# A gated short convolution beside attention: from channels in the rows to tokens in the rows

## The chip, the cores and the metric

One Trainium2 chip, and of it one core. The metric is the device time of one execution in microseconds. TensorE (PE in the profile) multiplies, VectorE (DVE), ScalarE (ACT) and GpSimd (POOL) do the elementwise work, and SyncE (SP) issues the weight loads.

## The reference

One decoder sub-layer over 256 tokens and a width of 2048, all in float32. The input is normalised and projected by one wide matrix; the columns feed a latent attention of 16 heads and a gated convolution of 3 taps. Both results are projected, merged by sigmoid gates, projected once more, normalised and added to the input.

```python
h = _rmsnorm(x, pre_norm_g)
proj = jnp.einsum('bsd,de->bse', h, w_in)
...
attn = attn.reshape(b, s, MLA_WIDTH) * jax.nn.silu(z_mla)
y_mla = jnp.einsum('bse,ed->bsd', attn, w_o_mla)

u = c_gate * c_in
u_pad = jnp.pad(u, ((0, 0), (CONV_K - 1, 0), (0, 0)))
conv = sum(conv_w[k] * u_pad[:, k:k + s] for k in range(CONV_K))
y_conv = jnp.einsum('bse,ed->bsd', b_gate * conv * jax.nn.silu(z_conv), w_o_conv)

merged = jax.nn.sigmoid(g_mla) * y_mla + jax.nn.sigmoid(g_conv) * y_conv
out = jnp.einsum('bsd,de->bse', merged, w_out)
x = x + _rmsnorm(out, post_norm_g)
```

## The kernel before

**Numbers in two halves.** Every float32 operand of a matmul is split into a high part (rounded to the matmul's type) and a low part (the rest): `split_act` writes the high part on ACT and the low part on DVE. A product is then three matmuls, high x high, high x low and low x high. `product` issues them one by one. `halves` puts the two halves of the activations side by side (`x_both`, 512 columns for 256 tokens), so that one matmul of 512 columns with the high weights and one of 256 with the low weights do the same; `whole` adds the two halves of the result.

**Weights.** They come in units of 128 x 2048 numbers (1 MB), loaded by SP into three `raw` buffers in the order of the list `plan`, and are split in halves of 1024 columns into five `whi` and five `wlo` buffers. `take(u)` hands out a unit and sees to it that the next one is split and three are loaded.

**Order.** TensorE's instructions stand in the order of the text (`keep_in_program_order`), and so do a few others. The rest of each engine's queue is ordered by the library's scheduler with a simulated timeline. `keep_in_program_order` queues an instruction behind the one written before it on its engine.

**Stages.** First the latents `qa` and `ckv` and the rotary key, with the normalisation of the input. Then 16 heads. For each head: the gate `z`; the attention's scores (`scores`), the turning of the probabilities (`turn`) and the values (`values`), and every head half a group of per-head projections (`group_a`, `group_b`); and between these four projections of 128 convolution channels, `cg`, `ci`, `b` and `c` in the profile (c_gate, c_in, b_gate, z_conv). Channels stand in the rows, tokens in the columns, so a shift in time is an offset in the columns: `u` has two zero columns ahead, and the three taps are one ACT and two DVE instructions. `cv_f` holds the result. In head 0 `latent_turn` transposes the latents between `z` and the first convolution unit.

Then the merged stage, `tokens(c, n, cols)`: for four blocks of 512 output columns the two gates (n = 0, 1, from `x_both`), the attention's output projection (n = 2, from `at_both`) and the convolution's (n = 3, from `cv_both`), with tokens in the rows; `features` turns the merged block. In the first block `split_branch` splits attention (n = 0) and convolution (n = 1). Last the output projection (`out`).

**Banks.** Of the eight accumulator banks, four rotate under `mm`, and `sm`, `sc`, `tp` and `o` are one each: for head 0's `ckv` transposes (`sm`, `sc`), scores, transposed probabilities and values.

Of the kernel before, what the change touches and what calls it, by code (L numbers as in the profile page):

```python
# [44 lines left out]
for _name, _n in (  # L45
    ("pre_g", KD), ("q_g", KR), ("kv_g", KR),
    ("cw0", KD), ("cw1", KD), ("cw2", KD), ("freq", 1), ("sign", 1),
):
    PV[_name] = (_at, _n)
    _at += _n  # L50
# [29 lines left out]
@with_exitstack  # L80
def tile_layer(ctx: ExitStack, tc: tile.TileContext, xw, x, pos, pvec, post_g, wc, wi, wkr, wqk, wrv, wsq, out):
    nc = tc.nc
# [13 lines left out]
    row_r = [top.tile([P, LINE], F32, name=f"frr{t}")[:, :1] for t in range(NT)]  # L96
    top.tile([P, 120], F32, name="top_pad")
    wpool = ctx.enter_context(tc.tile_pool(name="wpool", bufs=1))
# [5 lines left out]
    def add(ap, width=UNIT):  # L104
        plan.append((ap, width))
        return len(plan) - 1

    n_wi = 0

    def add_wi():  # L110
        nonlocal n_wi
        n_wi += 1
        return add(wi[n_wi - 1])

# [14 lines left out]
    for i, j in order:  # L129
        if j == "a":  # L130
            u_grp[i][0] = add(wqk[i])
        elif j == "b":
            u_grp[i][1] = add(wrv[i], 3 * HALF // 2)
        else:
            u_head[i][j] = add_wi()

# [119 lines left out]
    nc.scalar.activation(warm[:, :], mhalf[:, :], AF.Sigmoid)  # L256
    idle = bank("idle", tag="sm", bufs=1)
    for _ in range(9):
# [20 lines left out]
    kr = bp.tile([P, 2, S], F32R, name="kr")  # L279
    bp.tile([P, 4 * LINE], F32, name="bp_pad")  # L280
    mask = bp.tile([P, 3 * P], F32, name="mask")
# [60 lines left out]
    def input_rows(dgs):  # L342

        rb = bank("rb", tag="sm", bufs=1)
        for t in range(NT):
            matmul(rb[:, t * P : (t + 1) * P], ones[:, :], dgs[t][:, :], start=True, stop=True)
        nc.scalar.activation(r_x[:, :], rb[:, :S], AF.Copy)
# [103 lines left out]
    def latent_turn(name, both, g, tags):  # L451
        f = lat_f[name]
        for j2 in range(2):
            ps = bank(f"lt_{name}{j2}", tag=tags[j2], bufs=1)
            for j in range(2):
                for t in range(NT):
                    o, b = j * S + t * P, 2 * j2 + j
                    transpose(ps[:, o : o + P], f[:, t, b * P : (b + 1) * P], ident[:, :])
            for j in range(2):
                b, src = 2 * j2 + j, ps[:, j * S : (j + 1) * S]  # L460
                nc.scalar.activation(both[:, b, :S], src, AF.Copy, scale=col(g, b))
                nc.vector.scalar_tensor_tensor(
                    both[:, b, S:], src, col(g, b), both[:, b, :S].bitcast(F32), op0=ALU.mult, op1=ALU.subtract
                )
# [62 lines left out]
    def group_b(g):  # L527
        qr, vv = temp("qr", (P, HG, S), F32R), pair("vv", (P, NT, HG * DV), 2)
        w = take(u_grp[g][1])
        f = narrow(f"qr{g}", w, 0, qa)  # L530
        rope(f[:, :], f[:, :])
        for j in range(HG):

            own, other = (slice(DR * i, DR * i + DR) for i in (j, 1 - j))
            split_act(qr[own, j, :], qr[other, j, :], f[own, :])
        for t in range(NT):
            ps = bank(f"vv{g}_{t}")
            for k in range(KR):
                c = [ckv[:, k, o + t * P : o + (t + 1) * P] for o in (0, S)]
                product(ps[:, :S], c, w(2 + k, HG * DV), k == 0, k == KR - 1)  # L540
            split_act(vv[0][:, t, :], vv[1][:, t, :], ps[:, :S])
        groups[g] += [qr, vv]

    def scores(h):

        qn, kn, qr, _ = groups[h // HG]
        j = h % HG
        sc = bank(f"sc{h}", tag="sc", bufs=1)
        t0, t1 = slice(0, P), slice(P, S)
# [9 lines left out]
        if h == 0:  # L559
            temp("pad", (P, 3 * LINE), bufs=1)  # L560
        p = temp("p", (P, 3 * P), bufs=1)
# [23 lines left out]
    def turn(h, p):  # L585

        tp = bank(f"tp{h}", tag="tp", bufs=1)
        for b in range(3):
            transpose(tp[:, b * P : (b + 1) * P], p[:, b * P : (b + 1) * P], ident[:, :])
        pt = temp("pt", (P, 2, 3 * P), F32R, 1)  # L590
        split_act(pt[:, 0, :], pt[:, 1, :], tp[:, : 3 * P])
        return pt
# [15 lines left out]
    def silu(name, ps):  # L608
        f, s = temp("sl_f", bufs=1), temp(name, bufs=2 if name == "sz" else 1)
        whole(f[:, :], ps)  # L610
        rows(f[:, :])
        nc.scalar.activation(s[:, :], f[:, :], AF.Sigmoid)
        nc.vector.tensor_tensor(s[:, :], f[:, :], s[:, :], op=ALU.mult)
        return s

    def values_next(h):

        g, second = divmod(h, HG)
        if g + 1 < NG:
            (group_b if second else group_a)(g + 1)  # L620

    for h in range(H):
        uz, ug, ui, ub, uc = u_head[h]
        sz = silu("sz", project(uz, f"z{h}"))
        if h == 0:
            latent_turn("qa", qa, "q_g", ("tp", "o"))
            latent_turn("ckv", ckv, "kv_g", ("sm", "sc"))
            next(table_parts)
            key_rope()
        else:  # L630
            if h == 1:
                values(0, pt, sz0)
            p = scores(h)
        cg = temp("cg", bufs=1)
        whole(cg[:, :], project(ug, f"cg{h}"))
        rows(cg[:, :])
        if h == 0:
            group_a(0)
            group_b(0)
        u = temp("u", (P, S + 2), bufs=1)  # L640
        nc.gpsimd.memset(u[:, :2], 0.0)
        whole(u[:, 2:], project(ui, f"ci{h}"))
        nc.vector.tensor_tensor(u[:, 2:], u[:, 2:], cg[:, :], op=ALU.mult)
        rows(u[:, 2:])
        if h > 0:
            pt = turn(h, p)
        c = temp("c", bufs=1)
        nc.scalar.activation(c[:, :], u[:, :S], AF.Copy, scale=col("cw0", h))
        for i in (1, 2):
            nc.vector.scalar_tensor_tensor(  # L650
                c[:, :], u[:, i : i + S], col(f"cw{i}", h), c[:, :], op0=ALU.mult, op1=ALU.add
            )
        b = temp("b", bufs=1)
        whole(b[:, :], project(ub, f"b{h}"))
        nc.vector.tensor_tensor(c[:, :], b[:, :], c[:, :], op=ALU.mult)
        rows(c[:, :])
        if h > 0:
            values(h, pt, sz)
            values_next(h)
        else:  # L660
            p = scores(h)
        sg = silu("sg", project(uc, f"c{h}"))
        nc.vector.tensor_tensor(cv_f[:, h, :], c[:, :], sg[:, :], op=ALU.mult)
        if h == 0:
            values_next(h)
            pt, sz0 = turn(h, p), sz
# [7 lines left out]

    def split_branch(both, f, i):

        for h in (4 * i, 4 * i + 2):
            hs = slice(h, h + 2)
            split_act(both[:, hs, :S], both[:, hs, S:], f[:, hs, :], True)

    def tokens(c, n, cols):

        pss = [bank(f"sq{c}_{n}_{t}") for t in range(NT)]
        for kk in range(4):
            w = take(u_d[c][n][kk])
            if c == 0 and n < 2:
                split_branch(*((at_both, at_f), (cv_both, cv_f))[n], kk)
            for t in range(NT):
                for k4 in range(4):
                    k = 4 * kk + k4  # L690
                    a = [cols[:, k, o + t * P : o + (t + 1) * P] for o in (0, S)]
                    product(pss[t][:, :], a, w(k4, 512), k == 0, k == KD - 1)
        return pss
# [4 lines left out]
    def features(c, m, m_both):  # L698

        for t in range(NT):  # L700
            tp = bank(f"mt{c}_{t}", tag=("tp", "o")[t], bufs=1)
            for j in range(4):
                transpose(tp[:, j * P : (j + 1) * P], m[t][:, j * P : (j + 1) * P], ident[:, :])
            ks, ts = slice(4 * c, 4 * c + 4), slice(t * P, (t + 1) * P)
            lo = slice(t * P + S, (t + 1) * P + S)
            split_act(m_both[:, ks, ts], m_both[:, ks, lo], tp[:, :].rearrange("p (k q) -> p k q", k=4))

    waiting = m_both = None
    for c in range(4):
        gates = []  # L710
        for n in range(2):
            pss = tokens(c, n, x_both)
            if c == 0 and n == 1:
                fstack.close()
                merged_pool = ctx.enter_context(tc.tile_pool(name="merged_pool", bufs=1, side="right"))
                m_both = merged_pool.tile([P, KD, 2 * S], F32R, name="m_both")
            if waiting is not None:
# [8 lines left out]
        m = gates[0]  # L726
        pss = tokens(c, 2, at_both)
        for t in range(NT):
            nc.vector.tensor_tensor(m[t][:, :], pss[t][:, :], m[t][:, :], op=ALU.mult)
# [160 lines left out]
```

## Time and profile before

| | |
|---|---|
| median of 3 runs | 1058.01 us (1057.88 to 1059.24) |
| the profiled execution | 1058.48 us, span 1056.7 us |
| granted TensorE clock | 0.998 |
| heads (about 53 to 610 us) | 557 us |
| merged stage (610 to 961 us) | 351 us |
| output projection and end (961 to 1056.7 us) | 96 us |

The span is the time from the first to the last instruction; the execution's own time has a little around it. In the groups of the profile a row reads: line, engine, operation, written tile <- read tiles, shapes, count, busy time, mean time of one in ns, and the idle time before them with what ended it. In the chain of waits a row is start, length and what ran. `PEld` is the loading of TensorE's stationary operand, which overlaps the matmuls.

### The profile page before, as it was taken

How to read it: one execution, taken by the hardware profiler on the slowest of the kernel's cores; microseconds unless marked ns; L12 is line 12 of the kernel's file. 1: busy time of each engine (PE TensorE's matmuls, PEld its weight loads, DVE VectorE, ACT ScalarE, POOL GpSimd, SP SyncE). 2: the span in 40 equal slices, each digit the busy share in tenths (PEclk: the TensorE clock that was granted, in tenths of full speed). 3: DMA queues.
4: the chain of work that ended last, by engine and by line, in shares of the span. 5: the costliest groups of instructions: out<-in, count | busy, mean ns of one | idle time of the engine just before them, and what ended most of it. 6: DMA issues, size and time to landing. Idle time of an engine off the chain costs nothing.

```text
span 1056.7 us, 14237 instructions
## 1 busy us (share of the span) xinstructions
PE 1047.0 (99%) x5510; PEld 903.2 (85%) x5510; DVE 706.1 (67%) x1114; ACT 587.9 (56%) x858; POOL 44.1 (4%) x107
## 2 busy tenths in 40 slices
PE   9999999999999999999999999999999999999997
PEld 8888888988889888898888888888888888888885
DVE  7589877877878768778787766455554455445562
ACT  7777566666656666666665665334444434433450
POOL 7610000000000000000000000000000000000000
PEclk9999999999999999999999999999999999999999
DMA  8745454554545545454454555555555555558542
GB/s 341 303 166 189 160 200 150 199 199 150 180 171 192 187 166 195 167 188 174 176 188 171 187 175 197 198 199 175 189 194 199 197 187 187 187 199 308 190 179 80
DMA packets 29860, 201.81 MB, mean 191 GB/s; under 512 B 3360, under 2 KB 4064, under 8 KB 7392
## 3 DMA queue, kind: packets, MB, share of 16 engines
q1 hardware_dynamic: 29232, 197.54, 52.2%
q10 hardware_dynamic: 432, 3.33, 0.8%
q8 instruction: 43, 0.70, 0.3%
q14 instruction: 25, 0.20, 0.1%
q0 software_dynamic: 128, 0.03, 0.0%
HBM read 198.79 MB, written 2.10 MB: 190 GB/s over the span
## 4 chain that ended last, share of the span: by engine, by line
PE 98%; issue 1%; DVE 1%; POOL 0%; ACT 0%; POOLq 0%; DVEq 0%; ACTq 0%
PE sq L86 33%; PE ci L86 8%; PE b L86 8%; PE z L86 8%; PE c L86 8%; PE cg L86 8%; PE out L86 7%; PE vv L86 2%; PE qa L86 2%; PE ckv L86 2%; PE kn L86 2%; PE qn L86 2%; PE sc L86 1%; PE qr L86 1%; PE o L86 1%
## 5 line engine op out<-in xcount | busy, mean ns | idle before, releaser
L231 DVE TENSOR_TENSOR wlo<-raw,whi 128x1024 fp32r<-128x1024 f32 (+1 forms) x370 | 436.7, 1198 | 226.8 <-ACT whi L230 189.7
L230 ACT ACTIVATE whi<-raw 128x1024 fp32r<-128x1024 f32 (+1 forms) x372 | 383.6, 1035 | 334.2 <-PE sq L86 184.8
L86 PE MATMUL sq<-whi,x_both 128*128 128x512 f32 x512 | 159.0, 390 | 0.0
L86 PEld LDWEIGHTS sq<-whi,x_both 128*128 128x128 f32 x512 | 96.1, 188 | 19.8
L86 PE MATMUL sq<-wlo,x_both 128*128 128x512 f32 x256 | 99.6, 389 | 0.0
L86 PE MATMUL sq<-whi,cv_both 128*128 128x512 f32 x256 | 79.4, 389 | 0.0
L86 PE MATMUL sq<-whi,at_both 128*128 128x512 f32 x256 | 79.4, 389 | 0.0
L86 PE MATMUL out<-whi,m_both 128*128 128x512 f32 x256 | 79.3, 390 | 0.0
L86 PE MATMUL b<-x_both,whi 128*128 128x512 f32 x256 | 62.5, 396 | 0.0
L86 PE MATMUL z<-x_both,whi 128*128 128x512 f32 x256 | 61.2, 391 | 0.0
L86 PE MATMUL ci<-x_both,whi 128*128 128x512 f32 x256 | 61.1, 391 | 0.0
L86 PE MATMUL c<-x_both,whi 128*128 128x512 f32 x256 | 61.0, 390 | 0.0
L86 PE MATMUL cg<-x_both,whi 128*128 128x512 f32 x256 | 60.8, 390 | 0.0
L86 PEld LDWEIGHTS sq<-whi,cv_both 128*128 128x128 f32 x256 | 48.1, 188 | 10.0
L86 PEld LDWEIGHTS sq<-whi,at_both 128*128 128x128 f32 x256 | 48.1, 188 | 10.0
L86 PEld LDWEIGHTS out<-whi,m_both 128*128 128x128 f32 x256 | 48.1, 188 | 9.9
L86 PEld LDWEIGHTS sq<-wlo,x_both 128*128 128x128 f32 x256 | 48.1, 188 | 9.9
L86 PEld LDWEIGHTS ci<-x_both,whi 128*128 128x128 f32 x256 | 47.0, 188 | 9.2
L86 PEld LDWEIGHTS b<-x_both,whi 128*128 128x128 f32 x256 | 46.9, 188 | 9.3
L86 PEld LDWEIGHTS z<-x_both,whi 128*128 128x128 f32 x256 | 47.0, 188 | 9.1
L86 PEld LDWEIGHTS c<-x_both,whi 128*128 128x128 f32 x256 | 47.0, 188 | 9.1
L86 PEld LDWEIGHTS cg<-x_both,whi 128*128 128x128 f32 x256 | 47.0, 188 | 8.9
(223 smaller groups left out, 1550.6 us busy)
## 6 DMA issues: line engine op xcount, KB each, us to landing
raw<-wi_dram SPq DMA_DIRECT2D x80, 1024.0 KB, 4.8
raw<-wsq_dram SPq DMA_DIRECT2D x80, 1024.0 KB, 4.8
raw<-wqk_dram SPq DMA_DIRECT2D x8, 1024.0 KB, 4.8
raw<-wrv_dram SPq DMA_DIRECT2D x8, 768.0 KB, 4.1
raw<-wc_dram SPq DMA_DIRECT2D x4, 1024.0 KB, 10.0
cv_f<-x_dram SPq DMA_DIRECT2D x1, 2048.0 KB, 9.4
xr<-x_dram ACTq DMA_DIRECT2D x1, 2048.0 KB, 11.4
raw<-xw_dram SPq DMA_DIRECT2D x5, 384.0 KB, 6.0
```

The costliest lines, as they stand in the source:

```text
L86: return tc.keep_in_program_order(nc.tensor.matmul(*a, **kw))
L230: a = nc.scalar.activation(hi, src, AF.Copy)
L231: b = nc.vector.tensor_tensor(lo, src, hi.bitcast(F32), op=ALU.subtract)
```

## The change

The convolution's projections are made with tokens in the rows. Four heads share a block of 512 channels, and head h does one of the block's four projections, c_gate, c_in, z_conv and b_gate in turn: `channels(h, i)` takes its unit i (of 4) at the place where one of the four old projections stood, into two `cv` banks, one for each 128 tokens. `channels_done` evicts and multiplies as the projections come. Once u = c_gate * c_in is there, `taps` moves it down by one and by two rows with DMAs from POOL's queue, fetches the tap weights as rows broadcast to all partitions, and sums up, in steps (`yield`) that the loop calls later in the next head, with the sums on DVE kept in program order. In the merged stage `turn_branch` transposes the result on TensorE, at n = 1 and 2 of the first block, in place of the splits at n = 1.

The banks become four `mm`, two `cv`, one `st` (scores, transposed probabilities, and what used `sm`) and `o`; `latent_turn` uses `st` and `o` for `qa` and the two `cv` for `ckv`. Some tiles have one buffer instead of two, padding tiles change, and the tap weights leave the first small load `pvec`. The weight units keep their number, size and order; those of the convolution are laid out as the merged stage's.

```diff
-            u_head[i][j] = add_wi()
+            u_head[i][j] = add(wcv[i, j - 1] if j else wz[i])
...
-        qr, vv = temp("qr", (P, HG, S), F32R), pair("vv", (P, NT, HG * DV), 2)
+        qr, vv = temp("qr", (P, HG, S), F32R, 1), pair("vv", (P, NT, HG * DV))
...
-        sc = bank(f"sc{h}", tag="sc", bufs=1)
+        sc = bank(f"sc{h}", tag="st", bufs=1)
...
-        tp = bank(f"tp{h}", tag="tp", bufs=1)
+        tp = bank(f"tp{h}", tag="st", bufs=1)
...
+    cv_t = cv_f[:, :, :].rearrange("p (j t k) s -> p j t (k s)", j=4, t=NT)
+    cv_ps = {}
+
+    def channels(h, i):
+        if i == 0:
+            cv_ps["now"] = [bank(f"cv{h}_{t}", tag="cv", bufs=2) for t in range(NT)]
+        w = take(u_head[h][1 + i])
+        for t in range(NT):
+            for k4 in range(4):
+                k = 4 * i + k4
+                a = [x_both[:, k, o + t * P : o + (t + 1) * P] for o in (0, S)]
+                product(cv_ps["now"][t][:, :], a, w(k4, 512), k == 0, k == KD - 1)
+        if i == 3:
+            channels_done(*divmod(h, 4))
+
+    def channels_done(j, n):
+        for t in range(NT):
+            ps, r = cv_ps["now"][t], r_col[:, t : t + 1]
+            w, u = cv_w[:, t, :], cv_t[:, j, t, :]
+            if n == 0:
+                nc.scalar.activation(u, ps[:, :], AF.Copy, scale=r)
+            elif n == 2:
+                nc.scalar.activation(w, ps[:, :], AF.Sigmoid, scale=r)
+            if n:
+                dst = u if n == 1 else w
+                nc.vector.scalar_tensor_tensor(dst, ps[:, :], r, dst, op0=ALU.mult, op1=ALU.mult)
+            if n == 3:
+                nc.vector.tensor_tensor(u, u, w, op=ALU.mult)
+
+    def taps(j, t):
+        u, parts = cv_t[:, j, t, :], []
+        for d in (1, 2):
+            m = temp(f"mv{d}", (P, 512), bufs=1, tag=f"mv{d}x")
+            if t:
+                nc.gpsimd.dma_start(out=m[:d, :], in_=cv_t[P - d :, j, 0, :])
+            else:
+                nc.gpsimd.memset(m[:d, :], 0.0)
+            nc.gpsimd.dma_start(out=m[d:, :], in_=u[: P - d, :])
+            parts.append(m[:, :])
+        def tap(d):
+            cw = temp("cw", (P, 512), bufs=2)
+            nc.gpsimd.dma_start(out=cw[:, :], in_=cwr[2 - d : 3 - d, 512 * j : 512 * (j + 1)].to_broadcast([P, 512]))
+            return cw
+
+        def join(dst, a, b, op):
+            tc.keep_in_program_order(nc.vector.tensor_tensor(dst, a, b, op=op))
+
+        cws = [tap(d) for d in (1, 2)]
+        yield
+        for a, cw in zip(parts, cws):
+            join(a, a, cw[:, :], ALU.mult)
+        join(parts[0], parts[0], parts[1], ALU.add)
+        cw = tap(0)
+        yield
+        join(u, u, cw[:, :], ALU.mult)
+        join(u, u, parts[0], ALU.add)
+        yield
...
     for h in range(H):
...
         if h == 0:
-            latent_turn("qa", qa, "q_g", ("tp", "o"))
-            latent_turn("ckv", ckv, "kv_g", ("sm", "sc"))
+            latent_turn("qa", qa, "q_g", (("st", 1), ("o", 1)))
+            latent_turn("ckv", ckv, "kv_g", (("cv", 2), ("cv", 2)))
...
             p = scores(h)
-        cg = temp("cg", bufs=1)
-        whole(cg[:, :], project(ug, f"cg{h}"))
-        rows(cg[:, :])
+        channels(h, 0)
...
+        channels(h, 1)
         if h > 0:
             pt = turn(h, p)
...
+        if h % 4 > 1:
+            next(tap)
+        channels(h, 2)
         if h > 0:
             values(h, pt, sz)
+            if h % 4 > 1:
+                next(tap)
             values_next(h)
...
+        channels(h, 3)
+        if h % 4 in (1, 2):
+            tap = taps(h // 4, 2 - h % 4)
+            next(tap)
...
+    def turn_branch(i):
+        j, t = divmod(i, NT)
+        turned(f"ct{i}", cv_t[:, j, t, :], cv_both, j, t)
+
+    def turned(name, src, both, c, t):
+        tp = bank(name, tag=("st", "o")[t], bufs=1)
+        for j in range(4):
+            transpose(tp[:, j * P : (j + 1) * P], src[:, j * P : (j + 1) * P], ident[:, :])
+        ks, ts = slice(4 * c, 4 * c + 4), slice(t * P, (t + 1) * P)
+        lo = slice(t * P + S, (t + 1) * P + S)
+        split_act(both[:, ks, ts], both[:, ks, lo], tp[:, :].rearrange("p (k q) -> p k q", k=4))
...
-            if c == 0 and n < 2:
-                split_branch(*((at_both, at_f), (cv_both, cv_f))[n], kk)
+            if c == 0 and n == 0:
+                split_branch(kk)
+            if c == 0 and n in (1, 2):
+                turn_branch(4 * (n - 1) + kk)
```

More of the change, by code (lines that the diff above doesn't have):

```diff
@@ L46 @@
     ("pre_g", KD), ("q_g", KR), ("kv_g", KR),
-    ("cw0", KD), ("cw1", KD), ("cw2", KD), ("freq", 1), ("sign", 1),
+    ("freq", 1), ("sign", 1),
 ):
@@ L80, in tile_layer @@
 @with_exitstack
-def tile_layer(ctx: ExitStack, tc: tile.TileContext, xw, x, pos, pvec, post_g, wc, wi, wkr, wqk, wrv, wsq, out):
+def tile_layer(ctx: ExitStack, tc: tile.TileContext, xw, x, pos, pvec, post_g, wc, wz, wcv, wkr, wqk, wrv, cwr, wsq, out):
     nc = tc.nc
@@ L96, in tile_layer @@
     row_r = [top.tile([P, LINE], F32, name=f"frr{t}")[:, :1] for t in range(NT)]
-    top.tile([P, 120], F32, name="top_pad")
+    top.tile([P, 184], F32, name="top_pad")
     wpool = ctx.enter_context(tc.tile_pool(name="wpool", bufs=1))
@@ L106, in add @@
         return len(plan) - 1
[L108 to L113, printed above, removed]
     u_qa = [add(xw[i], 2 * XW) for i in range(KD // 2)]
@@ L256, in tile_layer @@
     nc.scalar.activation(warm[:, :], mhalf[:, :], AF.Sigmoid)
-    idle = bank("idle", tag="sm", bufs=1)
+    idle = bank("idle", tag="st", bufs=1)
     for _ in range(9):
@@ L279, in tile_layer @@
     kr = bp.tile([P, 2, S], F32R, name="kr")
-    bp.tile([P, 4 * LINE], F32, name="bp_pad")
     mask = bp.tile([P, 3 * P], F32, name="mask")
@@ L342, in input_rows @@
     def input_rows(dgs):
-        rb = bank("rb", tag="sm", bufs=1)
+        rb = bank("rb", tag="st", bufs=1)
         for t in range(NT):
@@ L453, in latent_turn @@
         for j2 in range(2):
-            ps = bank(f"lt_{name}{j2}", tag=tags[j2], bufs=1)
+            ps = bank(f"lt_{name}{j2}", tag=tags[j2][0], bufs=tags[j2][1])
             for j in range(2):
@@ L559, in scores @@
         if h == 0:
-            temp("pad", (P, 3 * LINE), bufs=1)
+            temp("pad", (P, 4 * LINE), bufs=1)
         p = temp("p", (P, 3 * P), bufs=1)
@@ L608, in silu @@
     def silu(name, ps):
-        f, s = temp("sl_f", bufs=1), temp(name, bufs=2 if name == "sz" else 1)
+        f, s = temp("sl_f", bufs=1), temp(name)
         whole(f[:, :], ps)
@@ L622, in tile_layer @@
+    cv_w = bp.tile([P, NT, 512], F32, name="cv_w")
     for h in range(H):
-        uz, ug, ui, ub, uc = u_head[h]
-        sz = silu("sz", project(uz, f"z{h}"))
+        sz = silu("sz", project(u_head[h][0], f"z{h}"))
         if h == 0:
-            latent_turn("qa", qa, "q_g", ("tp", "o"))
-            latent_turn("ckv", ckv, "kv_g", ("sm", "sc"))
+            latent_turn("qa", qa, "q_g", (("st", 1), ("o", 1)))
+            latent_turn("ckv", ckv, "kv_g", (("cv", 2), ("cv", 2)))
             next(table_parts)
@@ L639, in tile_layer @@
             group_b(0)
[L640 to L644, printed above, removed]
+        channels(h, 1)
         if h > 0:
             pt = turn(h, p)
[L647 to L656, printed above, removed]
+        if h % 4 > 1:
+            next(tap)
+        channels(h, 2)
         if h > 0:
             values(h, pt, sz)
+            if h % 4 > 1:
+                next(tap)
             values_next(h)
@@ L661, in tile_layer @@
             p = scores(h)
-        sg = silu("sg", project(uc, f"c{h}"))
-        nc.vector.tensor_tensor(cv_f[:, h, :], c[:, :], sg[:, :], op=ALU.mult)
+        channels(h, 3)
+        if h % 4 in (1, 2):
+            tap = taps(h // 4, 2 - h % 4)
+            next(tap)
         if h == 0:
@@ L673, in tile_layer, with split_branch @@
     dp = main.enter_context(tc.tile_pool(name="dp", bufs=1))
-    def split_branch(both, f, i):
+    def split_branch(i):
         for h in (4 * i, 4 * i + 2):
             hs = slice(h, h + 2)
-            split_act(both[:, hs, :S], both[:, hs, S:], f[:, hs, :], True)
+            split_act(at_both[:, hs, :S], at_both[:, hs, S:], at_f[:, hs, :], True)
+    def turn_branch(i):
[8 more added lines that the diff above has]
+        split_act(both[:, ks, ts], both[:, ks, lo], tp[:, :].rearrange("p (k q) -> p k q", k=4))
     def tokens(c, n, cols):
@@ L700, in features @@
         for t in range(NT):
[L701 to L706, printed above, removed]
+            turned(f"mt{c}_{t}", m[t], m_both, c, t)
     waiting = m_both = None
@@ L712, in tile_layer @@
             pss = tokens(c, n, x_both)
[L713 to L716, printed above, removed]
             if waiting is not None:
@@ L727, in tile_layer @@
         pss = tokens(c, 2, at_both)
+        if c == 0:
+            fstack.close()
+            merged_pool = ctx.enter_context(tc.tile_pool(name="merged_pool", bufs=1, side="right"))
+            m_both = merged_pool.tile([P, KD, 2 * S], F32R, name="m_both")
         for t in range(NT):
@@ L831 @@
     )
-    heads = np.stack([_cols(z), _cols(c_g), _cols(c_in), _cols(b_g), _cols(z_c)], axis=1)
-    wi = heads.reshape(-1, P, D)
     wq = w_q_b.reshape(R, H, DN + DR)
@@ L850 @@
         "pre_g": _feat(arr(pre_norm_g)), "q_g": _feat(arr(q_a_norm_g)), "kv_g": _feat(arr(kv_a_norm_g)),
-        "cw0": _feat(conv_w[0]), "cw1": _feat(conv_w[1]), "cw2": _feat(conv_w[2]),
         "freq": np.tile(freq, 4)[:, None],
@@ L867 @@
         "wc": c_kv.reshape(4, 4, P, R).transpose(0, 2, 1, 3).reshape(4, P, UNIT),
-        "wi": wi,
+        "wz": _cols(z),
+        "wcv": np.stack([
+            w.reshape(4, 4, P, 4, 512).transpose(3, 0, 2, 1, 4).reshape(4, 4, P, UNIT)
+            for w in (c_g, c_in, z_c, b_g)
+        ], axis=1).reshape(H, 4, P, UNIT),
         "wkr": np.ascontiguousarray(k_r.reshape(KD, P, DR).transpose(1, 0, 2)).reshape(P, KD * DR),
@@ L871 @@
         "wrv": np.ascontiguousarray(wrv),
+        "cwr": np.ascontiguousarray(conv_w),
         "wsq": np.stack([
```

## The prediction

> **What bounds the kernel now.** I read the page first (busy shares), then the busy time by stretch, then the chain that ended last, and last the timeline of the first head.
>
> ```profile
> PE 1047.0 (99%) x5510; PEld 903.2 (85%) x5510; DVE 706.1 (67%) x1114; ACT 587.9 (56%) x858; POOL 44.1 (4%) x107
> ...
> q1 hardware_dynamic: 29232, 197.54, 52.2%
> ```
>
> ```profile
> 101.00:610.00 509.00, 509.00 (x3045) 454.42 (x3044) 395.50 (x741) 321.92 (x518) 1.39 (x14) 1.00 0.51 178
> 610.00:719.00 109.00, 109.00 (x484) 90.24 (x483) 62.97 (x67) 53.61 (x63) 0.00 (x0) 1.00 0.54 193
> ```
>
> TensorE (PE) is busy for all 509 us of heads 1 to 15 and all of the first merged block, at a granted clock of 1.00. VectorE (DVE) has 78% of the attention stretch, ScalarE (ACT) 63%, the DMA engines 51%. So the change is worth what it takes off or puts on the matmul stream, plus any stretch in which TensorE has to wait. Nothing that DVE, ACT or the weight queue saves counts by itself.
>
> **The matmul stream, removed and added.** The chain of waits gives the pace of each kind of work:
>
> ```profile
> 141.70 5.55 PE cg L86 x32
> 147.25 5.57 PE ci L86 x32
> ...
> 153.14 5.59 PE b L86 x32
> ...
> 164.92 5.57 PE c L86 x32
> ...
> 610.08 108.83 PE sq L86 x480
> ...
> 806.84 0.87 PE mt L89 x8
> ```
>
> Now, one head's four convolution projections cost 5.55 + 5.57 + 5.59 + 5.57 = 22.28 us; each is 16 matmuls of 512 columns (weights stationary, both halves of x moving) and 16 of 256. Afterwards each unit is 24 matmuls of 512 columns with x stationary and the weights moving. That is the form of the merged stage's gate products, and there 480 take 108.83 us, 0.2267 us each, so a unit is 5.44 us and a head's four are 21.77. Saved: 0.51 us a head, over 16 heads **-8.2 us**. This needs no new estimate: same tiles, same shapes, same loop.
>
> Added on TensorE: the convolution result stands with tokens in the rows and has to be turned, 8 pieces of 4 transposes, put in front of units in the first merged block. The chain has 8 such transposes at 0.87 us, so 32 cost **+3.5 us**, all on the path, since the chain there is TensorE without a gap. The shift by one and two tokens, which was an offset in the columns and cost nothing on TensorE, becomes DMA and DVE work and costs nothing on TensorE either.
>
> Stream alone: -8.2 + 3.5 = -4.7 us.
>
> **The first head.** Here the change moves banks. The transposes of the key/value latent went to the banks `sm` and `sc`; now they go to the two `cv` banks, and the next thing on TensorE, the first convolution unit, needs just these two. Now it doesn't wait:
>
> ```profile
> 59.42 0.95 PE lt_ckv L89 x8
> 60.37 5.56 PE cg L86 x32
> 65.92 1.41 PE qn L86 x8
> ...
> 72.60 1.40 PE qr L86 x8
> ...
> 76.87 5.76 PE ci L86 x32
> ```
>
> When do the two banks come free? The evictions, ACT and then DVE:
>
> ```profile
> 62.30 0.87 ACT L461 ACTIVATE qa<-lt_qa,pv 128x256 fp32r<-128x256 f32 x2 [0.29 <-DVE qa L462]
> 63.08 0.47 ACT L461 ACTIVATE ckv<-lt_ckv,pv 128x256 fp32r<-128x256 f32 x1
> ...
> 65.71 0.46 ACT L461 ACTIVATE ckv<-lt_ckv,pv 128x256 fp32r<-128x256 f32 x1
> ```
>
> ```profile
> 62.57 0.48 DVE L462 SCALAR_TENSOR_TENSOR ckv<-lt_ckv,pv,ckv 128x256 fp32r<-128x256 f32 x1
> ...
> 64.47 0.47 DVE L462 SCALAR_TENSOR_TENSOR ckv<-lt_ckv,pv,ckv 128x256 fp32r<-128x256 f32 x1
> ...
> 66.20 0.48 DVE L462 SCALAR_TENSOR_TENSOR ckv<-lt_ckv,pv,ckv 128x256 fp32r<-128x256 f32 x1 [0.46 <-ACT ckv L461]
> ```
>
> The first row shows ACT waiting for DVE on `lt_qa`: in one bank the two engines take turns, ACT, DVE, ACT, DVE. So the pieces of the first `lt_ckv` bank are the DVE one at 62.57, the ACT one that starts as it ends (63.08) and the DVE one at 64.47. That bank is free at 64.94 and the second at 66.68. The first convolution unit, ready at 60.37, would start 64.94 - 60.37 = **4.6 us late**. Its second half starts 12 matmuls (2.7 us) later, at 67.7, when the second bank is free. Bounds: four evictions in series with nothing between take 0.46 + 0.48 + 0.47 + 0.48 = 1.9 us, and waiting for the very last one, at 66.68, costs 6.3. I take 4.6, because the order on ACT and DVE up to there depends on nothing that the change touches.
>
> Against it, some idle time goes. From 65.92 to 72.60 TensorE did two `qn` and two `kn` products, all four of the same 8 matmuls, 4 x 1.41 = 5.64 us of work in 6.68. The missing 1.04 us is mostly the last `kn`, which waited for a bank:
>
> ```profile
> 70.93 1.19 PE L86 MATMUL kn<-ckv,whi 128*128 128x512 f32 x4 [0.80 <-DVE cg L354]
> ```
>
> It waited for `cg` to leave its `mm` bank. `cg` no longer sits in `mm`, and DVE catches up during the new wait, so I drop the 1.04, and the 0.19 that this `ci` unit took over 5.57: **-1.2 us**, with 0 as the other end if the later evictions are still behind. Start together: +3.4 us.
>
> **DVE, ACT and the weight buffers.** Evictions and gating of a 4-head block fall from 56 small DVE instructions to 8 wide ones, plus 10 wide ones for the taps. I cost this at nothing, since TensorE waits for neither. The cover to watch is the lead of the weight halves:
>
> ```profile
> L231 DVE TENSOR_TENSOR wlo<-raw,whi 128x1024 fp32r<-128x1024 f32 x352 | 424.2, 1224 | 220.0 <-ACT whi L230 189.7 <-PE c L86 10.4 <-PE ci L86 8.5
> ```
>
> ```profile
> L230 ACT ACTIVATE whi<-raw 128x1024 fp32r<-128x1024 f32 x352 | 371.5, 1058 | 327.7 <-PE sq L86 184.8 <-PE b L86 24.4 <-PE out L86 22.1
> L612 ACT ACT_TABLE_LOAD x17 | 21.8, 1283 | 0.3
> ...
> L723 ACT ACTIVATE sg<-sq,r_both 128x512 f32<-128x512 f32 x16 | 11.0, 689 | 8.2 <-PE sq L86 8.2
> ```
>
> Five buffers hold 2.5 units. In the new order a half is read for both token tiles, so the first is given back after 18 of 24 matmuls, 4.08 us into a unit, and the half that takes its place is needed two units later, after 6 matmuls: 2 x 5.44 + 1.36 - 4.08 = 8.2 us. Splitting takes 1.06 + 1.22 = 2.3 us, so DVE or ACT may fall 5.9 us behind before TensorE notices. The merged stage has this pattern and lost nothing.
>
> The two `cv` banks carry no spare: a block of 512 channels leaves them while TensorE does the next head's `z` (5.57) and scores (0.95), 6.5 us. The longest eviction, of the conv gate, is a table load 1.28, two sigmoids at 0.69 and a DVE product each; the first bank's can begin 2.7 us before the block ends. It is free about 3 us after the block's end even if one weight split stands ahead: no stall, 0, with up to 1 us x 4 as the other end.
>
> **The shifts.** Eight times (4 blocks, 2 token tiles) POOL's queue takes two shift copies of 127 and 126 rows of 2 KB, their carried rows or memsets, and three tap rows broadcast from memory; `join`, pinned on DVE behind everything traced before it, waits for them, and behind it queue the weight splits for which TensorE waits. Nothing of this size is in the trace on POOL's queue; the nearest are
>
> ```profile
> L370 POOL DMA_DIRECT2D ta_i<-pos_dram x4: 506/511/731, 1.8 to 3.5; - x4
> ...
> DMA to landing us min/median/max: 4.7/5.4/5.7
> ```
>
> Call T the end of the block's second projection. DVE's two products end by about T + 2, six issues at 0.5 us and 5.4 to landing give T + 10.5. The join can't run before TensorE has done z, scores, two units and the turn: 5.57 + 0.95 + 10.88 + 0.33, T + 17.7. So 7 us of slack, then 5.9 us of cover: 0 us; what is later than both, TensorE pays, and the first rival is the bound on that side. In all they move 8 x 5 x 0.26 = 10.4 MB, 5% more traffic on engines that are half idle; SP's queue of weights keeps its number and size of loads.
>
> **Sum.** The profiled execution took 1058.48 us (span 1056.7 and 1.8 around it). -8.2 + 3.5 + 4.6 - 1.2 = -1.3, 1057.2; the median of the runs is 0.47 lower (1058.01), so **1056.7 us**. That is a tenth of a per cent less, where the measurement tells about 0.2% (2.1 us) from no change.
>
> **Rivals.** *The shift lands late (slower).* If a copy of 127 rows is carried by one DMA engine: 197.54 MB kept 16 engines busy 52.2% of 1056.7 us, 44.7 engine-us per MB, so 0.26 MB takes 11.6 us alone, and 24.3 us beside the weights, which hold 52% of that engine. It would land at T + 27, 9 us after the join's turn, 3.2 us more than the cover; on the first tap set of each of 4 blocks (the second can be issued a head before) +13 us: **1069.7**. It decides from a landing at T + 24 on. Against it, the copies may be spread, and alone on its engine one hides. The Trainium skill's "DMA: Bandwidth & Descriptors", section "Why a DMA increments its semaphore by 16 and not by 1", says that the engine count divides the row count, so that 127 rows get one engine, and names an exception in which POOL's direct copies are spread over all 16; no row here shows which. Chance 0.14.
>
> *The wait at the start is short (faster).* If the evictions of `lt_ckv` are queued ahead of the rest, it falls to 1.9 us: **1054.0**. For it, DVE and ACT order is made anew for the changed program; against it, `z` and `lt_qa`, written before, come first in the trace. Chance 0.17.
>
> *The clock falls in that wait.* TensorE has not been idle over 1.1 us since its start, and the clock is 1.00 throughout; after 4.6 us it might be granted half for a while. One unit at half clock costs 5.4 us more: **1062.1**; half a unit, 1059.4. The skill's "TensorE: Matmul & The Clock Gate", "Part 1: The HAM clock gate", has such a fall after an idle window of about 3.4 us, and as long a busy one to come back: by that, an estimate of 1.7 us more. Chance 0.09.
>
> *Evictions or joins a little late in many blocks*, 0.3 us in each of 16: **1061.5**; chance 0.08.
>
> **How the numbers follow.** The forecast has 0.52; its own range is 1055.2 (wait 3.1) to 1058.4 (wait 6.3), 0.14 of it below 1055.9. Faster by over 0.2%: 0.14 + 0.17 = 0.31. Slower: 0.14 + 0.04 (half of the clock's) + 0.08 = 0.26. Within: 0.43. Range: from the short wait's 1054.0 less 0.6 for the unknown ends to 1063, which takes in the clock and leaves out the late shift.
>
> **What would show it.** In the changed profile: convolution units at 5.44 us; 32 transposes named `ct` at 0.11 us each; TensorE idle about 4.6 us before the first convolution unit, put down to DVE's `ckv`, and no wait for `cg`; DVE waits for the DMA of `mv` tiles near zero. Units still at 5.57 us, a wait there under 2 us, or TensorE waiting for weight splits behind a `join` would make the prediction wrong.

## The result and the profile after

| | before | after |
|---|---|---|
| median (5 runs each) | 1058.22 us (1057.88 to 1059.24) | 1062.91 us (1061.91 to 1063.69) |
| profiled execution, span | 1058.48, 1056.7 us | 1061.91, 1060.1 us |

The ratio is 1.0042, 95% interval 1.0027 to 1.0057: slower by 0.4%. The prediction was 1056.7, no change that can be told. The time is at the edge of the range (0.1 us below its upper end of 1063), and the sign is wrong.

The page after, its busy shares and the queue of the shifts:

```profile
PE 1045.5 (99%) x5030; PEld 880.2 (83%) x5030; DVE 670.8 (63%) x962; ACT 563.5 (53%) x778; POOL 71.7 (7%) x147
...
q0 software_dynamic: 3584, 10.50, 3.7%
```

Busy time by stretch, as shown of before, with one more row for the first head (53 to 101 us), which is given of before too, ahead of the three of after. Columns: stretch, length, then busy time (instructions) of PE, PEld, DVE, ACT, POOL, the granted clock, DMA share, GB/s:

```profile
53.00:101.00 48.00, 47.20 (x286) 41.90 (x286) 42.82 (x87) 34.64 (x62) 4.59 (x13) 1.00 0.52 181
```

```profile
53.00:101.00 48.00, 43.02 (x224) 36.77 (x224) 34.78 (x65) 27.52 (x49) 6.26 (x15) 0.96 0.48 170
101.00:610.00 509.00, 509.00 (x2603) 434.82 (x2602) 368.50 (x613) 304.80 (x456) 28.86 (x54) 1.00 0.59 200
610.00:719.00 109.00, 109.00 (x497) 90.20 (x496) 62.50 (x64) 52.68 (x60) 0.00 (x0) 1.00 0.52 184
```

TensorE is busy for all of heads 1 to 15 here too. Most of the loss is in the first head: TensorE is busy for 43.0 of 48 us, where it was 47.2, and the clock's mean there is 0.96. The chain of waits, in order of time:

```profile
66.91 7.09 PE cv L86 x24
74.00 2.78 PE qn L86 x16
76.78 2.81 PE kn L86 x16
79.58 1.41 PE qr L86 x8
...
147.71 10.89 PE cv L86 x48
158.93 5.48 PE cv L86 x24
...
170.58 5.49 PE cv L86 x24
...
609.74 21.76 PE sq L86 x96
631.51 0.44 PE ct L89 x4
631.95 5.50 PE sq L86 x24
```

The first convolution unit (`cv`, 24 matmuls) starts at 66.91 instead of 60.37 and takes 7.09 us; later ones take 5.45 to 5.49. The timeline says what it waited for, and how much later the `z` product ahead of it already began (before: 52.74, the first row is of before, the others of after; the last is the eviction that it waited for):

```profile
52.74 3.89 PE L86 MATMUL z<-x_both,whi 128*128 128x512 f32 x16
```

```profile
54.10 3.89 PE L86 MATMUL z<-x_both,whi 128*128 128x512 f32 x16
...
66.91 0.77 PE L86 MATMUL cv<-whi,x_both 128*128 128x512 f32 x1 [4.72 <-DVE ckv L455]
```

```profile
66.28 0.47 DVE L455 SCALAR_TENSOR_TENSOR ckv<-lt_ckv,pv,ckv 128x256 fp32r<-128x256 f32 x1
```

The granted clock, us by us (third column from the end):

```profile
65.00:66.00 1.00, 0.00 (x0) 0.00 (x0) 1.00 (x4) 0.98 (x2) 0.00 (x0) 1.00 0.87 369
66.00:67.00 1.00, 0.10 (x1) 0.13 (x1) 0.76 (x2) 0.99 (x3) 0.00 (x0) 0.75 0.00 0
67.00:68.00 1.00, 1.00 (x3) 0.81 (x4) 0.88 (x3) 0.46 (x2) 0.00 (x0) 0.50 0.00 0
68.00:69.00 1.00, 1.00 (x4) 0.81 (x3) 0.95 (x3) 0.00 (x0) 0.00 (x0) 0.50 0.00 0
69.00:70.00 1.00, 1.00 (x4) 0.76 (x4) 0.95 (x3) 0.00 (x0) 0.00 (x0) 0.54 0.00 0
70.00:71.00 1.00, 1.00 (x6) 0.84 (x5) 0.51 (x2) 0.42 (x1) 0.00 (x0) 1.00 0.00 0
```

The clock falls at 66.5, still in the wait, and stays at half for 3.4 us; TensorE works in about 3.0 of them. Where the 3.4 us between the two profiled executions come from:

| step | forecast | measured | from |
|---|---|---|---|
| late start of `z` | 0 | +1.4 | 54.10 against 52.74 |
| wait for the `cv` banks | +4.6 | +5.2 | its start, 66.91 against 60.37, less the 1.4 above; 4.72 idle before it and 0.25 in `lt_ckv` |
| the first unit, with its half clock | -0.1 | +1.5 | 7.09 against 5.56 |
| wait of the last `kn` | -1.0 | -1.1 | 5.58 against 6.68 from `qn` to `qr` |
| the other 63 units, and the 0.19 of `ci` | -8.3 | -7.3 | from `qr` to the merged stage, 530.2 against 537.5 |
| merged stage to the end of TensorE's part of the chain | +3.5 | +3.9 | 431.9 against 428.0 |

Unrounded, the measured steps add up to 3.5; what follows took 0.1 less.

### The profile page after: what moved, and what is told of

It reads as the page before. It is cut to its first block, busy times and chain, and to the rows that moved or that the text cites. A ratio compares the mean times of both kernels' runs of the same rounds, so it can differ in the third digit from the quotient of the medians.

```text
span 1060.1 us, 13095 instructions
## 1 busy us (share of the span) xinstructions
PE 1045.5 (99%) x5030; PEld 880.2 (83%) x5030; DVE 670.8 (63%) x962; ACT 563.5 (53%) x778; POOL 71.7 (7%) x147
## 4 chain that ended last, share of the span: by engine, by line
PE 93%; DMA 2%; POOL 2%; issue 2%; DVE 1%; ACT 0%; SPq 0%; POOLq 0%; DVEq 0%; ACTq 0%
PE cv L86 33%; PE sq L86 33%; PE z L86 8%; PE out L86 7%; PE vv L86 2%; PE kn L86 2%; PE qn L86 2%; PE sc L86 1%; PE qr L86 1%; DMA cv_f<-xw_dram 1%; DMA raw<-wc_dram 1%; PE o L86 1%; POOL cos_t L406 1%; PE qa L86 1%; POOL sin_t L406 1%
## 5 line engine op out<-in xcount | busy, mean ns | idle before, releaser
L86 PE MATMUL cv<-whi,x_both 128*128 128x512 f32 x1024 | 326.3, 392 | 4.7 <-DVE ckv L455 4.7
L86 PEld LDWEIGHTS cv<-whi,x_both 128*128 128x128 f32 x1024 | 193.0, 188 | 44.0 <-issue 4.9
L86 PE MATMUL cv<-wlo,x_both 128*128 128x512 f32 x512 | 200.0, 391 | 0.0
L86 PEld LDWEIGHTS cv<-wlo,x_both 128*128 128x128 f32 x512 | 96.7, 189 | 18.6
L86 PE MATMUL sq<-wlo,at_both 128*128 128x512 f32 x128 | 49.8, 389 | 0.0
L86 PE MATMUL sq<-wlo,cv_both 128*128 128x512 f32 x128 | 49.8, 389 | 0.0
L86 PE MATMUL out<-wlo,m_both 128*128 128x512 f32 x128 | 49.8, 389 | 0.0
L86 PEld LDWEIGHTS z<-x_both,wlo 128*128 128x128 f32 x256 | 32.8, 191 | 1.2
```

Source lines behind the costliest of these rows:

```text
L86: return tc.keep_in_program_order(nc.tensor.matmul(*a, **kw))
```

## The experiments

**Theory**: the loss sits in the first head and has three parts: the wait for the banks, the fall of the clock that the wait brings, and a late start. **Rivals**: the wait is only moved when the banks are changed; the late start has another cause; the first unit is slow for another reason than the clock; the loss is spread.

**The latent's transposes in other banks (e1_banks).**

```diff
-            latent_turn("ckv", ckv, "kv_g", (("cv", 2), ("cv", 2)))
+            latent_turn("ckv", ckv, "kv_g", (("mm", 4), ("mm", 4)))
```

> The changed kernel, with the two ckv transposes of head 0 in the mm banks, so that the first convolution unit has its own banks free. Theory (the loss sits in the first head: 4.7 us of waiting for the cv banks, 1.65 us of half clock after it, about 1.4 us of a late start): the wait and the fall of the clock both go, 6.4 us, to about 1056.5 us; the start stays 1.4 us late. Rival (the wait is only moved: kn or qn then wait for the mm banks instead): 1059 to 1061, with TensorE idle before qn or kn. Rival (the loss is spread over the heads and the merged stage): no change, 1062.9.

Measured: 1056.59 us, 0.9982 of before (0.9973 to 0.9990). The chain of waits:

```profile
54.98 5.55 PE z L86 x32
60.53 0.87 PE lt_qa L89 x8
61.41 0.87 PE lt_ckv L89 x8
62.28 5.47 PE cv L86 x24
67.75 2.78 PE qn L86 x16
70.53 2.81 PE kn L86 x16
```

There is no gap from `z` to `kn` any more, the first unit takes 5.47 us, and the wait did not turn up elsewhere. The start is still late (54.98 in the chain, 54.73 by the timeline).

**The tap rows kept in order (e2_pin).** In the changed kernel the scheduler had moved the first two loads of tap rows, which depend on nothing, to the start of POOL's queue, beside the first loads of x and weights. The timeline of after, POOL:

```profile
3.99 1.10 POOL L659 DMA_DIRECT2D cw<-cwr_dram  x2
```

The DMA issues, size and median time to landing, before and then after:

```profile
cv_f<-xw_dram SPq DMA_DIRECT2D x2, 768.0 KB, 8.9
```

```profile
cv_f<-xw_dram SPq DMA_DIRECT2D x2, 768.0 KB, 11.0
```

```diff
-            nc.gpsimd.dma_start(out=cw[:, :], in_=cwr[...].to_broadcast([P, 512]))
+            tc.keep_in_program_order(
+                nc.gpsimd.dma_start(out=cw[:, :], in_=cwr[...].to_broadcast([P, 512]))
+            )
```

> The changed kernel, with the loads of the tap rows kept in program order on POOL's queue, so that the first two (512 KB) are not issued at 4 us among the first weight loads. Theory (they delay the loads of x and of the first weights): the first z product starts at 53.0 instead of 54.1 to 54.4 us, 1.4 us gained, about 1061.5 us. Rival (the start is late for another reason, such as the smaller first load or POOL's order): no change, z still at 54.1 or later.

Measured: 1061.50 us, 1.0027 (1.0018 to 1.0037). `z` starts at 53.17 and those loads land in 9.4 us, so 0.9 of the 1.4 us of late start comes from the hoisted loads. Up to there TensorE waited in the changed kernel twice, 0.8 us in all, for split weights of the first latent, which it did neither before nor in e2_pin:

```profile
PE qa L86 <- ACT whi L224: 0.8, 2, 0.6
```

The other 0.4 us stays open; in e2_pin the first four products took 1.65 us against 1.18 before. The first unit took longer than in the changed kernel, 8.22 us, because here the clock fell 1.4 us before the unit began (0.4 there) and stayed low for 6.8 us:

```profile
63.00:64.00 1.00, 0.00 (x0) 0.00 (x0) 1.00 (x4) 0.98 (x3) 0.00 (x0) 1.00 0.98 418
64.00:65.00 1.00, 0.00 (x0) 0.00 (x0) 1.00 (x4) 1.00 (x1) 0.00 (x0) 0.53 0.38 156
```

Behind the same wait of 4.72 us the first unit thus took 1.6 us longer than a later one (5.47) in one profile and 2.8 in another.

**Both edits (e3_both).**

> Both edits: ckv transposes in the mm banks and the tap loads in program order. Theory: the two losses are separate and add, 7.8 us, about 1055.1 us, 0.3% under the kernel before; steady units of 5.45 us, 32 transposes of 3.5 us and no wait in head 0 left. Rival (they share a cause, one hides the other): no better than the bank edit alone, 1056.5.

Measured: 1054.27 us (1053.98 to 1055.03), 0.9962 (0.9949 to 0.9974): faster than both kernels. `z` starts at 52.57, and no wait of TensorE is left from there to the end of its work. The two losses are separate: together the edits gain 8.6 us, the banks alone 6.3 and the loads alone 1.4. Against e1_banks the loads are worth 2.3 us, 0.9 more than against the changed kernel; that e2_pin's longer half clock hides the rest is likely, but not shown. What remains is the change by itself: -4.4 us.

**The wait filled with idle products (e4_fill, e7_half_fill).**

```diff
+        if h == 0:
+            idle2 = bank("idle2")
+            for _ in range(20):
+                matmul(idle2[:, :P], ones[:, :], ones[:, :], start=True, stop=True)
         channels(h, 0)
```

In e7_half_fill the loop is `range(9)`.

> The changed kernel, with 20 idle products of 128 columns on TensorE between the ckv transposes and the first convolution unit, in an mm bank; they change no result. The wait for the cv banks stays, but TensorE is busy in most of it. Theory (the idle time itself makes the granted clock fall to half for about 3.3 us): the clock stays at 1.00 after the wait, the first unit takes 5.45 instead of 7.1 us, about 1061.2 us. Rival (the first unit is slow for its weights or its second bank, not for the clock): it still takes 7 us, 1062.9.

> As e4_fill, with 9 idle products instead of 20: TensorE is busy for about 2.0 of the 4.7 us of waiting and idle for 2.7. Theory (the fall needs an idle stretch longer than that): the clock stays at 1.00 and the time is e4_fill's, 1060.9 us. Rival (any idle stretch of some microseconds brings the fall): the first unit takes 7 us or more and the time is that of the changed kernel, 1062.9.

Measured: 1060.92 us (ratio 1.0024, 1.0016 to 1.0033) with 20, and 1062.99 (1.0040, 1.0027 to 1.0053) with 9. With 20 the clock stays at 1.00 and the first unit, behind a gap of 0.25 us, takes 5.72 us; so the slow first unit is the clock, not its weights or banks, and of its 7.09 and 8.22 us in the two profiles 1.4 and 2.5 are the clock. With 9, the theory failed. The timeline and the chain of e7_half_fill (an idle product stands there as two matmuls):

```profile
62.80 2.17 PE L86 MATMUL idle<-ones 128*128 128x128 f32 x18
67.69 0.47 PE L86 MATMUL cv<-whi,x_both 128*128 128x512 f32 x1 [2.71 <-DVE ckv L455]
```

```profile
67.69 7.34 PE cv L86 x24
```

2.7 us of idling were enough here: the clock fell 0.7 us after TensorE had started again, and stayed at half for 3.4 us.

**The wait alone, in the kernel before (e5_before_wait).**

```diff
-        whole(cg[:, :], project(ug, f"cg{h}"))
+        whole(cg[:, :], project(ug, f"cg{h}", **({"tag": "sm", "bufs": 1} if h == 0 else {})))
```

> The kernel before, with one thing done to it: head 0's cg product goes to the bank sm, which the first ckv transposes hold, so that it waits as the first convolution unit does in the changed kernel. Theory (the wait and the clock's fall after it are the whole loss of the first head and need nothing else of the change): TensorE waits 4.6 us, the cg product then runs part of its time at half clock, 1.7 to 2.8 us more, and the wait of the last kn for cg's bank (about 1 us) goes: 1058.7 + 5.3 to 6.4 = 1064.0 to 1065.1 us. Rival (the wait costs less, because the work behind it catches up): 1060 to 1062.

Measured: 1064.36 us, 1.0055 (1.0041 to 1.0069). The timeline shows the same 4.72 us, and the product takes 7.20 instead of 5.56 us:

```profile
65.88 5.29 PE L86 MATMUL cg<-x_both,whi 128*128 128x512 f32 x16 [4.72 <-DVE ckv L462]
```

So the loss needs nothing of the convolution's new form; one product in a bank that the latent's transposes hold is enough.

**Without the turn (e6_no_turn).**

```diff
-        turned(f"ct{i}", cv_t[:, j, t, :], cv_both, j, t)
+        ...
+        split_act(cv_both[:, ks, ts], cv_both[:, ks, lo], cv_t[:, j, t, :].rearrange("p (k q) -> p k q", k=4))
```

> The kernel of e3_both without the 32 transposes of the convolution: its numbers are split as they stand, not turned, so the convolution's output projection reads the wrong axis; everything else is done. Theory (the turn is all on the path, 8 x 0.44 us and about 0.04 us a unit beside it): 3.5 to 3.9 us less than e3_both's 1054.3, 1050.4 to 1050.8 us. Rival (part of it is hidden under waits): less than 2 us gained, above 1052.3.

Measured: 1050.96 us, 3.3 less than e3_both, where 3.5 to 3.9 had been expected. The chain has the first merged block in one piece:

```profile
602.07 108.80 PE sq L86 x480
```

In e3_both the same block with the turn, from 601.34 to 714.01, took 112.67 us, 3.9 more. The turn is on the path with all its time.

**The shifts landing late (e8_shift_twice).**

```diff
-            nc.gpsimd.dma_start(out=m[d:, :], in_=u[: P - d, :])
+            for _ in range(2):
+                nc.gpsimd.dma_start(out=m[d:, :], in_=u[: P - d, :])
```

> The kernel of e3_both with each of the two shift copies of 127 and 126 rows made twice, one behind the other; each second copy waits for the first, so the moved rows land about 12 us later. Theory (slack of some 7 us to the join, and 5.9 us that DVE may fall behind before TensorE runs out of split weights): DVE waits for the copies up to 5 us on the first tap set of each block, TensorE does not, 1054.3 us within 0.2%. Rival (the cover is smaller, so that a late join is paid for at once): 4 x 3 to 5 us, 1066 to 1074 us.

Measured: 1054.84 us, 0.9964 (0.9952 to 0.9977), as e3_both. The two chains of copies ran side by side, so the rows came 6 us later, not 12. POOL's second copies, and the first `join` on DVE, in head 2:

```profile
141.76 1.19 POOL L656 DMA_DIRECT2D mv<-cv_f  x2 [4.70 <-DMA mv<-cv_f]
```

```profile
153.89 1.29 DVE L666 TENSOR_TENSOR mv<-mv,cw 128x512 f32<-128x512 f32 x2
```

DVE waited for no copy even so. The join's turn comes about 20 us after the block's second projection (133.72), not 17.7. How late a join may be before TensorE pays was not reached, so the cover of 5.9 us stays an estimate.

## Why the prediction failed, step by step

**The stream of matmuls was right in kind, 1 us too good.** A unit takes 5.45 to 5.49 us, not 5.44: those that follow another kind of product, and the merged units behind a turn (5.48 to 5.50), are a little longer. By the rows shown a head saves 0.42 us instead of 0.51 (10.89 + 5.48 + 5.49 against 22.28), and the merged stage loses 3.9 instead of 3.5. The change by itself is worth -4.4 us, as e3_both shows, where the steps gave -5.9.

**The wait was right**: 4.6 forecast, 4.72 measured, from the order of ACT and DVE on the two banks: the unit began as the eviction ended that the prediction had named, and e5_before_wait has the same wait. The `kn` wait went as said.

**The clock was set at nothing, and that failed.** It was a rival with a chance of 0.09, with the argument that no idle stretch over 1.1 us had been seen; but an unseen case is not an unlikely one, and my own forecast held an idle stretch four times as long. It cost 1.4 us in one profile and 2.5 in another, 2.0 by the medians with and without the 20 idle products. From the Trainium skill's "TensorE: Matmul & The Clock Gate", "Part 1: The HAM clock gate", the prediction had estimated 1.7 us; the traces lie on both sides of it. The 2.7 us of idling in e7_half_fill are less than the idle window of 3.4 us that the Trainium skill states there, so here the measurement differs. That the time came out near this rival's 1062.1 is luck: its 5.4 us stood for a whole unit at half clock, and what the clock did not cost of them came from the late start, the smaller saving and the longer turn.

**The start was set at nothing, and that failed too.** I took the shift DMAs to be issued where the text has them. The loads of tap rows have no input that is written on the chip, so they could be issued at the beginning, and two were, at 4 us, where TensorE lives on fresh loads (the DMA share was 0.83 in the first 53 us). It cost 1.4 us by e2_pin, 2.3 by e1_banks against e3_both. The prediction weighed the bytes on average, 5% over the run, and not at their place.

**The late shift did not come.** Copies of 127 rows landed in 6.0 us, those of 126 in 5.7, where by the prediction's estimate one engine alone would have needed 11.6:

```profile
mv<-cv_f POOLq DMA_DIRECT2D x8, 254.0 KB, 6.0
mv<-cv_f POOLq DMA_DIRECT2D x8, 252.0 KB, 5.7
```

The DMA queues show it more plainly. In the changed kernel all packets of the first pair of copies moved between 146.8 and 149.0 us (packets, MB, and the share of the 16 engines there):

```profile
q0 software_dynamic: 160, 0.52, 65.6%
```

65.6% of 16 engines are as much as 10.5 of them for two copies, so neither was left to one engine. For 127 rows that agrees with the exception that the Trainium skill's "DMA: Bandwidth & Descriptors" names for POOL's direct copies, and not with the rule of one engine that stands there. The chance of 0.14 was spent in the wrong place.

## What to carry to other kernels

When tiles change banks, follow the next user of every bank in time: the gain of the 16 heads, some 7 us, was lost to a single wait in the first, with the half clock behind it (5.2 and 1.5 us). Price a wait of TensorE with the clock that may fall behind it. And of every DMA that is added ask what it depends on; if on nothing, it can be issued at the start, among the loads that the first product needs, unless it is held in order.

## What was not expected of the hardware

An idle stretch of 2.7 us was enough for half clock, and the same wait of 4.72 us gave 3.4 us of half clock in one profile and 6.8 in another. By the clock records of the traces half clock lasted 3.41 us in the changed kernel, in e5_before_wait and in e7_half_fill, and 6.83, twice as long, in e2_pin. In e2_pin the clock fell 3.3 us after TensorE had gone idle (4.3 in the changed kernel), and TensorE was busy in only 2.0 of the first 3.41 us at half clock; that the second stretch follows from this is not shown. So a kernel with one such wait varies: the five runs of the changed kernel lie between 1061.91 and 1063.69 us, and the profiled one, the fastest, has the highest mean clock (0.997, the others 0.995 to 0.996).
